# Linear attention's gate sums from edge rows by small DMAs, its steps reordered, and layer 0's denominators issued with the value matmuls

## The chip, the cores and the metric

The kernel runs on one core of a Trainium2 chip. The metric is device time in microseconds. The five engines each run their own instruction list in order: TensorE (PE, with its weight loads listed as PEld), VectorE (DVE), ScalarE (ACT), GpSimd (POOL) and SyncE (SP), which here issues most DMAs.

## The reference

A two-layer backbone over 2048 latent tokens and 256 context tokens of width 1024, all in float32. Layer 0 runs two groups of heads side by side: eight heads of softmax attention, and four heads of gated linear attention (GLA) in both directions. Layer 1 is a neighbourhood attention. The change lies in layer 0. GLA, for one direction, in chunks of tokens:

```python
def step(state, inp):
    qi, ki, vi, gi = inp                      # gi: log gates, one per key channel
    b = jnp.cumsum(gi, axis=-2)
    b_last = b[..., -1:, :]
    q_t, k_t = qi * jnp.exp(b), ki * jnp.exp(-b)
    att = jnp.where(mask, jnp.einsum('bhld,bhmd->bhlm', q_t, k_t), 0.0)
    o = jnp.einsum('bhld,bhde->bhle', q_t, state) + jnp.einsum('bhlm,bhme->bhle', att, vi)
    k_dec = ki * jnp.exp(b_last - b)
    state = state * jnp.exp(b_last)[..., 0, :, None] + jnp.einsum('bhld,bhle->bhde', k_dec, vi)
    return state, o
```

The softmax attention is the usual one: scores, exponential, sum over keys, value product, division by the sum (the denominator).

## The kernel before

All 2304 tokens stand as 18 tiles of 128, and GLA's chunk is one such tile. A tile framework traces the program and plans each engine's order from a modelled timeline: an instruction is placed when its inputs and a buffer are there in the model, those traced earlier first. `issue_after(x)` only keeps an instruction behind x on its engine. On the chip the lists are then fixed.

`even_mix` traces GLA's first pass and its scans (`gla`) and then softmax attention (`even_attention`), so the two are interleaved on all engines.

*Softmax attention.* Four pairs of heads `j`, each with a block of 256 context queries (2 key tiles) and four blocks of 512 queries (18 key tiles): 74 iterations for a pair, 296 in all. An iteration makes scores for two heads, three matmuls each (L1003 to L1005, tile `st`, three PSUM banks), two exponentials on ACT into `apt` (14 buffers), and two additions on DVE that sum the weights (L994, `acc`). Value matmuls (`tail`, L945, tile `av`, two banks) go out in groups: when six iterations are pending, four are issued (L1015). When a block's last value matmul has been issued, `late` receives the block with a countdown of iterations (L948); `step_late` counts down in every iteration (L1014), and at zero `finish` makes the denominators (L876, tile `den`, one bank), a logarithm and an exponential on ACT, three operations on DVE (L881 to L883, the last of which reads the `av` bank), and the gate on POOL (L885).

*GLA, first pass.* For a chunk, `front` loads its inputs `u`, makes three copies of the 32 low-rank gate inputs (POOL, L721), transposes them, makes gate logits and log gates `G` (one buffer). Then L739 makes cumulative sums `mid`, centred at the middle of the chunk, with the matrix `tri`. L743 makes the sums of each half of the chunk (four matmuls of two columns, weights `G`, moving `ind`), three activations take their exponentials into `fac`, and POOL multiplies them (L748). `qt` and `kt` (one buffer each) are the exponentials of `mid` and `-mid`, times q and k (L753). `back` transposes `qt` and `kt` (L766), makes scores (L776), masks them, makes the chunk's own output (L785), stored to DRAM, and the chunk's contribution to the state (L791), which DVE scales with `fac` into `D` (L792). All of it turns in two PSUM banks, tag `gl`. The three steps of `back` for a chunk alternate with the three of `front` for the next.

*GLA, scan and second pass.* `scan` runs over the 18 chunks, forward on POOL (half of the partitions) and backward on DVE (the other half), three operations a chunk (L814 to L816). The second pass multiplies the queries with each chunk's state (L835), normalises and gates. `hook` releases one step of it, and of the splitting of the next weights, in every fourth attention iteration from the 166th on.

SP issues all loads and stores of this stage in one list.

Of the kernel before, what the change touches and what calls it, by code (L numbers as in the profile page):

```python
# [10 lines left out]
F32 = mybir.dt.float32  # L11
# [77 lines left out]
class Kern:  # L89
# [596 lines left out]
    def gla(self, gp, gs, g1, gd, pp, tag):  # L686
# [5 lines left out]
        self.gO = self.scr("gO", (NT, P, 512), F32)  # L692
        raw = self.tl(gs, [P, 512], "ge")
# [7 lines left out]
        ind = self.tl(gp, [P, 2], "ind")  # L701
        nc.sync.dma_start(ind[:], self.i["halves"])
# [7 lines left out]
        fac = [self.tl(gp, [P, H, 3], f"fac{c}") for c in range(NT)]  # L710
# [3 lines left out]
        def front(c):  # L714

            u = self.tl(g1, [P, 1056], "gu")
            nc.sync.dma_start(u[:], self.Un[c, :, :1056])
            gq, gk, gv = u[:, :256], u[:, 256:512], u[:, 512:1024]
            ps = bank()
            u3 = self.tl(gs, [P, 3, 32], "gu3")  # L720
            g.tensor_copy(u3[:], u[:, 1024:1056].unsqueeze(1).to_broadcast([P, 3, 32]))  # L721
# [12 lines left out]
            nc.vector.scalar_tensor_tensor(out=G[:], in0=lg[:], scalar=0.0, in1=e[:], op0=ALU.min, op1=ALU.subtract)  # L734
            G4 = G[:].rearrange("p (h z d) -> p h z d", z=2, h=H)
            yield
            mid = bank()
            for z in range(2):
                nc.tensor.matmul(mid[:].rearrange("p (h z d) -> p h z d", z=2, h=H)[:, :, z, :], tri[:, z, :], G4[:, :, z, :], start=True, stop=True)  # L739
            hs = bank()  # L740
            hs4 = hs[:, : 2 * H].rearrange("p (h c) -> p h c", h=H)
            for h in range(H):
                nc.tensor.matmul(hs4[:, h, :], G[:, h * P : h * P + P], ind[:], start=True, stop=True)  # L743
            f = fac[c]
            self.act(f[:64, :, 0:2], hs4[:64], AF.Exp, scale=1 / 16)
            self.act(f[64:, :, 0], hs4[64:, :, 1], AF.Exp, scale=1 / 16)
            self.act(f[64:, :, 1], hs4[64:, :, 0], AF.Exp, scale=1 / 16)
            g.tensor_tensor(out=f[:, :, 2], in0=f[:, :, 0], in1=f[:, :, 1], op=ALU.mult)  # L748
            qt = self.tl(g1, [P, 512], "gqt", bufs=1)
            kt = self.tl(g1, [P, 512], "gkt", bufs=1)  # L750
            for dst, src, sc in ((qt, gq, 1 / 16), (kt, gk, -1 / 16)):
                self.act(dst[:], mid[:], AF.Exp, scale=sc)
                nc.vector.tensor_tensor(out=z4(dst[:]), in0=z4(dst[:]),  # L753
                                        in1=src.rearrange("p (h d) -> p h d", h=H).unsqueeze(2).to_broadcast([P, H, 2, 64]), op=ALU.mult)
            tiles[c] = gv, f, qt, kt
            yield

        def back(c):

            gv, f, qt, kt = tiles.pop(c)  # L760
# [7 lines left out]
            nc.sync.dma_start(self.gQ[c], qT[:].rearrange("p h t -> p (h t)"))  # L768
            yield
# [19 lines left out]
            ps = bank()  # L789
            for h in range(H):  # L790
                nc.tensor.matmul(ps[:, h * P : h * P + P], kt[:, h * P : h * P + P], gv[:, h * P : h * P + P], start=True, stop=True)  # L791
            nc.vector.tensor_tensor(out=Dl[c][:], in0=ps[:].rearrange("p (h t) -> p h t", h=H),  # L792
                                    in1=f[:, :, 1:2].to_broadcast([P, H, P]), op=ALU.mult)
            yield

        tiles = {}
        for _ in front(0):
            pass
        for c in range(NT):
            nxt = front(c + 1) if c + 1 < NT else iter(())  # L800
            for _ in back(c):
                next(nxt, None)

        def scan(order, sl, eng, name):
            S = None
            n = sl.stop - sl.start
            for c in order:
# [5 lines left out]
                else:  # L813
                    eng.tensor_tensor(out=N[sl], in0=S[sl], in1=f[sl, :, 2:3].to_broadcast([n, H, P]), op=ALU.mult)  # L814
                    eng.tensor_tensor(out=N[sl], in0=N[sl], in1=d[sl], op=ALU.add)  # L815
                    eng.tensor_tensor(out=d[sl], in0=S[sl], in1=f[sl, :, 0:1].to_broadcast([n, H, P]), op=ALU.mult)  # L816
# [72 lines left out]
    def even_attention(self, ap, pp, hook):  # L889
# [49 lines left out]
        def tail(j, nb, n, kt, pts):  # L939
# [7 lines left out]
            if n == len(kts) - 1:  # L947
                late.append([2 if nb else 5, j, nb])  # L948
# [15 lines left out]
        for j in range(4):  # L964
# [12 lines left out]
            for nb, (q0, w, kts) in enumerate(blocks):  # L977
# [18 lines left out]
                for n, kt in enumerate(kts):  # L996
# [823 lines left out]
```

## Time and profile before

| | us |
|---|---|
| median of 3 runs | 3648.87 (3647.48 to 3651.03) |
| profiled execution | 3651.72 |
| its span, first to last instruction | 3649.9 |
| mean granted TensorE clock | 0.985 |
| busy: PE / PEld / DVE / ACT / POOL | 3552.6 / 2750.0 / 2355.6 / 1433.1 / 1200.8 |

A row of the timeline gives start, duration, engine, line of the kernel, operation, tile written and tiles read, shapes, count, and in brackets how long the engine was idle before it and who released it. Matmuls overlap in their pipeline, so that the time from one start to the next says what one costs, not its duration. A float32 matmul shows as two records.

### The profile page before, as it was taken

Reading aid. Unit: us, or ns where it says so; the run is one execution under the profiler, and the core shown is the slowest. Engines: PE = TensorE matmul, PEld = TensorE weight load, DVE = VectorE, ACT = ScalarE, POOL = GpSimd, SP = SyncE. Lnnn points to the kernel's source line nnn. Section 1 sums busy time; section 2 is a strip of 40 time slices with the busy share of each in tenths; the row PEclk is TensorE's granted clock in tenths of the full one; section 3 lists DMA queues with packets and bytes.
Section 4 is the critical chain, followed back from the end, with each engine's and each line's share of the span. In section 5 each row is a group of like instructions: output and inputs, shape, how many; then the busy total and the mean of one; then the engine's idle time right before and its main releaser. Section 6 shows DMA issues by size and latency. Waiting matters only on the chain.

```text
span 3649.9 us, 51809 instructions
## 1 busy us (share of the span) xinstructions
PE 3552.6 (97%) x18404; PEld 2750.0 (75%) x18404; DVE 2355.6 (65%) x4860; ACT 1433.1 (39%) x2741; POOL 1200.8 (33%) x1336
## 2 busy tenths in 40 slices
PE   8999999999999999999999999999899999999899
PEld 6988998888886666665657878888688887555577
DVE  4677666888876666688664435545578784666721
ACT  5545551111115555555553224444422223555510
POOL 1433330101011222112311234333344434777743
PEclk9999999999999999999999999999999999999999
DMA  7455472222242232334533544445743437778554
GB/s 255 146 154 157 135 207 82 86 76 89 74 131 66 76 102 72 93 92 116 164 98 116 186 160 126 146 142 170 226 145 123 140 119 204 209 206 220 176 179 149
DMA packets 364372, 512.19 MB, mean 140 GB/s; under 512 B 25825, under 2 KB 243889, under 8 KB 358210
## 3 DMA queue, kind: packets, MB, share of 16 engines
q1 hardware_dynamic: 322642, 425.49, 39.5%
q0 software_dynamic: 19872, 55.92, 5.2%
q10 hardware_dynamic: 21600, 27.46, 2.1%
q8 instruction: 146, 2.39, 0.3%
q14 instruction: 112, 0.92, 0.1%
HBM read 329.38 MB, written 179.37 MB: 139 GB/s over the span
## 4 chain that ended last, share of the span: by engine, by line
PE 71%; issue 15%; DVE 5%; POOL 4%; DMA 4%; ACT 2%; POOLq 0%; SPq 0%; DVEq 0%; ACTq 0%
PE av L945 7%; PE gm L129 6%; PE gm L131 6%; PE gm L130 6%; PE st L1003 4%; PE st L1004 4%; PE st L1005 4%; PE o L1515 2%; PE st L129 2%; PE st L131 2%; PE st L130 2%; PE st L1482 2%; PE pj L129 2%; PE pj L131 2%; PE pj L130 2%
## 5 line engine op out<-in xcount | busy, mean ns | idle before, releaser
L994 DVE TENSOR_TENSOR acc<-acc,apt 128x512 f32<-128x512 f32 x512 | 368.7, 743 | 163.1 <-ACT apt L106 160.4
L106 ACT ACTIVATE apt<-st 128x512 f32<-128x512 f32 (+1 forms) x592 | 343.1, 593 | 290.8 <-PE st L1005 258.9
L662 DVE TENSOR_REDUCE mm<-mx 128x1 f32<-128x512 f32 (+1 forms) x656 | 393.0, 629 | 91.1 <-PE mx L661 82.8
L945 PE MATMUL av<-apt,av 128*64 128x512 f32 (+1 forms) x1184 | 279.1, 594 | 0.0
L1003 PE MATMUL st<-aq,akh 97*128 97x512 f32 x576 | 249.2, 433 | 4.2 <-ACT apt L106 4.2
L661 PE MATMUL mx<-mk,mq 96*128 96x512 f32 (+1 forms) x656 | 238.6, 372 | 0.0
L1004 PE MATMUL st<-aq,akh 96*128 96x512 f32 x576 | 230.0, 399 | 0.0
L1005 PE MATMUL st<-aq,akl 96*128 96x512 f32 x576 | 229.6, 399 | 0.0
L106 ACT ACTIVATE opt<-opt 128x930 f32<-128x930 f32 (+9 forms) x144 | 119.2, 830 | 247.9 <-POOL opt L1686 139.8
L1389 DVE CUSTOM_DVE_ANT_1 mx<-mx,mtab 128x217 f32<-128x217 f32 (+11 forms) x576 | 184.5, 338 | 49.5 <-PE mx L1383 37.0
L106 ACT ACTIVATE u<-gm 128x352 f32<-128x352 f32 (+1 forms) x144 | 70.3, 495 | 357.9 <-PE gm L131 208.2
L1646 DVE TENSOR_TENSOR opt<-st,tab 128x64 f32<-128x64 f32 (+10 forms) x576 | 142.8, 316 | 87.0 <-PE st L1483 60.7
L945 PEld LDWEIGHTS av<-apt,av 128*64 128x64 f32 x1184 | 80.4, 137 | 153.8 <-issue 152.2
L1521 POOL TENSOR_TENSOR oacc<-oacc,opt 128x682 f32<-128x682 f32 (+9 forms) x144 | 169.8, 1202 | 28.9 <-ACT opt L106 27.7
L1003 PEld LDWEIGHTS st<-aq,akh 97*128 97x128 f32 x576 | 109.3, 190 | 86.9 <-issue 45.0
L661 PEld LDWEIGHTS mx<-mk,mq 96*128 96x128 f32 x656 | 122.8, 188 | 11.7
L1005 PEld LDWEIGHTS st<-aq,akl 96*128 96x128 f32 x576 | 110.4, 192 | 25.4
L1004 PEld LDWEIGHTS st<-aq,akh 96*128 96x128 f32 x576 | 110.7, 192 | 17.5
L106 ACT ACTIVATE x<-px,modB,modA 128x128 f32<-128x128 f32 x272 | 99.1, 468 | 58.2 <-PE px L331 36.0
L1482 PE MATMUL st<-q,kt 128*128 128x480 f32 (+5 forms) x256 | 99.7, 391 | 22.5 <-DVE opt L1646 17.9
L815 POOL TENSOR_TENSOR gsf<-gsf,D 64x512 f32<-64x512 f32 x17 | 24.8, 1459 | 276.8 <-DVE D L792 276.8
L129 PE MATMUL gm<-w1h,hhi 128*128 128x512 f32 x288 | 115.1, 400 | 0.0
(576 smaller groups left out, 10020.6 us busy)
## 6 DMA issues: line engine op xcount, KB each, us to landing
q<-Q SPq DMA_DIRECT2D x48, 512.0 KB
H<-x ACTq DMA_DIRECT2D x36, 512.0 KB
adaw<-ada_w SPq DMA_DIRECT2D x64, 256.0 KB
x<-H SPq DMA_DIRECT2D x32, 512.0 KB
wraw<-w_od SPq DMA_DIRECT2D x64, 256.0 KB
K1t<-okt POOLq DMA_DIRECT2D x32, 512.0 KB, 7.7
kt<-K1t SPq DMA_DIRECT2D x32, 512.0 KB
mtab<-rpb_q SPq DMA_DIRECT2D x16, 899.0 KB
```

The lines of the kernel that those rows point to most:

```text
L106: return self.nc.scalar.activation(out, in_, func, **kw)
L129: self.nc.tensor.matmul(out, lh(k), rh(k), start=j == 0, stop=False)
L130: self.nc.tensor.matmul(out, lh(k), rl(k), start=False, stop=False)
L131: yield self.nc.tensor.matmul(out, ll(k), rh(k), start=False, stop=j == n - 1)
L661: mm = nc.tensor.matmul(ps[:, :w], q[:A_QK, (t % 6) * P : (t % 6) * P + P], k[:A_QK, k0 : k0 + w], start=True, stop=True)
L662: nc.vector.tensor_reduce(out=m[:, t, n : n + 1], in_=ps[:, :w], axis=AX.X, op=ALU.max)
L945: nc.tensor.matmul(O[j, nb][i * 64 : i * 64 + 64, :w], V[j, kt // TT][:, kt % TT, i * 64 : i * 64 + 64], pts[i][:, :w], start=n == 0, stop ...
L994: self.add = nc.vector.tensor_tensor(out=acc[i][:, :w], in0=a[:, :w], in1=pts[i][:, :w], op=ALU.add)
L1003: nc.tensor.matmul(ps[:, :w], kh[: A_QK + 1, i, kq], qh[: A_QK + 1, :w], start=True, stop=False)
L1004: nc.tensor.matmul(ps[:, :w], kh[:A_QK, i, kq], ql[:A_QK, :w], start=False, stop=False)
L1005: mm = nc.tensor.matmul(ps[:, :w], kl[:A_QK, i, kq], qh[:A_QK, :w], start=False, stop=True)
L1389: nc.vector.tensor_tensor_reduce(out=s, in0=s, in1=tb[:, ri : ri + rn, ci : ci + cn], scale=1.0, scalar=-3e38, op0=ALU.add, op1=ALU.max, a ...
```

## The change

The sums of the two halves of a chunk are already in the centred sums: the first and the last row of `exp(mid)` and `exp(-mid)` hold the exponentials of the halves' sums, up to the gate of the edge token itself. So the matmuls with `ind`, their bank and their activations go. Instead, two rows of `G`, one row each for two directions of `qt`, and two rows of `kt` are written to a small DRAM tensor `gE` before `qt` and `kt` are multiplied with q and k, and read back transposed into `fac`, one element per partition, head and kind. One exponential on ACT and two products on POOL finish the factors.

Around it the steps move. The multiplication with q and k goes from `front` to the start of `back`, and so does the load of `u`. The chunk's contribution to the state is made right after the transposes and copied by DVE; POOL multiplies it with its factor at the end of `back`. The three copies of the gate inputs come straight from a DMA. `front` runs up to two chunks ahead of `back`.

In softmax attention the countdown is 1 for every block, and `step_late` is called only when a value group goes out, ahead of it.

```diff
+        self.gE = self.scr("gE", (NT, 2, 3, 512), F32)
...
-        ind = self.tl(gp, [P, 2], "ind")
-        nc.sync.dma_start(ind[:], self.i["halves"])
...
-        fac = [self.tl(gp, [P, H, 3], f"fac{c}") for c in range(NT)]
+        fac = [self.tl(gp, [P, 4, H], f"fac{c}") for c in range(NT)]
...
         def front(c):
-            u = self.tl(g1, [P, 1056], "gu")
-            nc.sync.dma_start(u[:], self.Un[c, :, :1056])
-            gq, gk, gv = u[:, :256], u[:, 256:512], u[:, 512:1024]
             ps = bank()
             u3 = self.tl(gs, [P, 3, 32], "gu3")
-            g.tensor_copy(u3[:], u[:, 1024:1056].unsqueeze(1).to_broadcast([P, 3, 32]))
+            nc.sync.dma_start(u3[:], self.Un[c, :, 1024:1056].unsqueeze(1).to_broadcast([P, 3, 32]))
...
-            hs = bank()
-            hs4 = hs[:, : 2 * H].rearrange("p (h c) -> p h c", h=H)
-            for h in range(H):
-                nc.tensor.matmul(hs4[:, h, :], G[:, h * P : h * P + P], ind[:], start=True, stop=True)
-            f = fac[c]
-            self.act(f[:64, :, 0:2], hs4[:64], AF.Exp, scale=1 / 16)
-            self.act(f[64:, :, 0], hs4[64:, :, 1], AF.Exp, scale=1 / 16)
-            self.act(f[64:, :, 1], hs4[64:, :, 0], AF.Exp, scale=1 / 16)
-            g.tensor_tensor(out=f[:, :, 2], in0=f[:, :, 0], in1=f[:, :, 1], op=ALU.mult)
+            nc.sync.dma_start(self.gE[c, :, 2], G[0::127])
...
+            self.act(qt[:], mid[:], AF.Exp, scale=1 / 16)
+            for z, t in enumerate((127, 0)):
+                nc.sync.dma_start(self.gE[c, z : z + 1, 0], qt[t : t + 1])
+            self.act(kt[:], mid[:], AF.Exp, scale=-1 / 16)
+            nc.sync.dma_start(self.gE[c, :, 1], kt[0::127])
+            tiles[c] = qt, kt
+            yield
+
+        def back(c):
+            qt, kt = tiles.pop(c)
+            u = inputs.pop(c)
+            f = fac[c]
+            for z in range(2):
+                nc.sync.dma_start(f[z * 64 : z * 64 + 64, :3, :].rearrange("p n h -> p (n h)"),
+                                  self.gE[c, z].rearrange("n (h z d) -> z d (n h)", z=2, h=H)[z])
+            for dst, src in ((qt, gq), (kt, gk)):
                 nc.vector.tensor_tensor(out=z4(dst[:]), in0=z4(dst[:]), ...
...
             nc.sync.dma_start(self.gQ[c], qT[:].rearrange("p h t -> p (h t)"))
+            ps = bank()
+            for h in range(H):
+                nc.tensor.matmul(ps[:, h * P : h * P + P], kt[:, h * P : h * P + P], gv[:, h * P : h * P + P], start=True, stop=True)
+            nc.vector.tensor_copy(Dl[c][:].rearrange("p h t -> p (h t)"), ps[:])
             yield
...
             nc.sync.dma_start(self.gO[c], oi[:])
-            ps = bank()
-            for h in range(H):
-                nc.tensor.matmul(ps[:, h * P : h * P + P], kt[:, h * P : h * P + P], gv[:, h * P : h * P + P], start=True, stop=True)
-            nc.vector.tensor_tensor(out=Dl[c][:], in0=ps[:].rearrange("p (h t) -> p h t", h=H),
-                                    in1=f[:, :, 1:2].to_broadcast([P, H, P]), op=ALU.mult)
+            self.act(f[:, 2, :], f[:, 2, :], AF.Exp, scale=1 / 16)
+            g.tensor_tensor(out=f[:, 1, :], in0=f[:, 1, :], in1=f[:, 2, :], op=ALU.mult)
+            g.tensor_tensor(out=f[:, 3, :], in0=f[:, 0, :], in1=f[:, 1, :], op=ALU.mult)
+            g.tensor_tensor(out=Dl[c][:], in0=Dl[c][:], in1=f[:, 0, :].unsqueeze(2).to_broadcast([P, H, P]), op=ALU.mult)
             yield
...
-        for c in range(NT):
-            nxt = front(c + 1) if c + 1 < NT else iter(())
-            for _ in back(c):
-                next(nxt, None)
+        def fetch_u(c):
+            if c < NT:
+                inputs[c] = self.tl(g1, [P, 1056], "gu")
+                nc.sync.dma_start(inputs[c][:, :1024], self.Un[c, :, :1024])
+
+        tiles, inputs = {}, {}
+        fr = [front(c) for c in range(NT)] + [iter(())] * 2
+        fetch_u(0)
+        for c in (0, 0, 1, 0, 1):
+            next(fr[c])
+        for c in range(NT):
+            fetch_u(c + 1)
+            b = back(c)
+            for x in (b, fr[c + 2], fr[c + 1], b, fr[c + 2], b):
+                next(x, None)
...
             if n == len(kts) - 1:
-                late.append([2 if nb else 5, j, nb])
+                late.append([1, j, nb])
...
                     with self.tc.issue_after(mm.ins):
-                        step_late()
                         if len(pend) == 6:
+                            step_late()
                             for _ in range(4):
                                 tail(*pend.pop(0))
```

More of the change, by code (lines that the diff above doesn't have):

```diff
@@ L813, in scan @@
                 else:
-                    eng.tensor_tensor(out=N[sl], in0=S[sl], in1=f[sl, :, 2:3].to_broadcast([n, H, P]), op=ALU.mult)
+                    eng.tensor_tensor(out=N[sl], in0=S[sl], in1=f[sl, 3, :].unsqueeze(2).to_broadcast([n, H, P]), op=ALU.mult)
                     eng.tensor_tensor(out=N[sl], in0=N[sl], in1=d[sl], op=ALU.add)
-                    eng.tensor_tensor(out=d[sl], in0=S[sl], in1=f[sl, :, 0:1].to_broadcast([n, H, P]), op=ALU.mult)
+                    eng.tensor_tensor(out=d[sl], in0=S[sl], in1=f[sl, 1, :].unsqueeze(2).to_broadcast([n, H, P]), op=ALU.mult)
                 S = N
```

10 lines of the change are left out of this document (1 added, 9 removed).

## The prediction

> **What bounds it now.** I read the page first: the engines' shares, then the chain that ended last, then the DMA queues.
>
> ```profile
> PE 3552.6 (97%) x18404; PEld 2750.0 (75%) x18404; DVE 2355.6 (65%) x4860; ACT 1433.1 (39%) x2741; POOL 1200.8 (33%) x1336
> ...
> q1 hardware_dynamic: 322642, 425.49, 39.5%
> ...
> PE 71%; issue 15%; DVE 5%; POOL 4%; DMA 4%; ACT 2%; POOLq 0%; SPq 0%; DVEq 0%; ACTq 0%
> ```
>
> TensorE is busy for 97% of the span and holds most of the chain. The change touches layer 0's attention with the linear attention inside it, about 1084 to 1965 us, so I asked for busy time by stretches of 50 us there. Columns: stretch, its length, then PE, PEld, DVE, ACT and POOL busy, granted clock, DMA share, GB/s.
>
> ```profile
> 1300.00:1350.00 50.00, 50.00 (x262) 31.60 (x260) 32.33 (x48) 27.50 (x59) 11.52 (x12) 1.00 0.38 109
> ...
> 1650.00:1700.00 50.00, 45.83 (x202) 27.61 (x200) 45.94 (x69) 24.96 (x48) 9.47 (x9) 0.93 0.28 85
> ```
>
> At 1300 us PE has no gap, with DVE at 65% and ACT at 55%: here a microsecond of PE work removed is a microsecond off the end, and work moved to DVE, ACT, POOL or DMA is hidden while its queue isn't late. The second row is the exception: PE loses 4.2 us, the clock falls to 0.93, and DVE is at 92%.
>
> Next the instructions on the linear attention's PSUM banks, `gl` (duration min/median/max, then first and last start):
>
> ```profile
> L743 PE MATMUL gl<-ind,gG x144: 167/251/272, 1122.6 to 1583.4; 128*128 128x2 f32 x144
> L739 PE MATMUL gl<-gG,tri x72: 377/379/483, 1121.7 to 1579.6; 128*128 128x256 f32 x72
> ```
>
> The removed half-chunk sums are L743: 72 matmuls, two records each, four matmuls in each of 18 chunks. L739, which stays, gives the pace: (1579.6 - 1121.7) / 17 = 26.9 us a chunk.
>
> **1. The half-chunk matmuls go.** Their durations overlap, so the price is read from starts:
>
> ```profile
> 1312.14 0.40 PE L1005 MATMUL st<-aq,akl 96*128 96x512 f32 x1
> 1312.38 0.95 PE L743 MATMUL gl<-ind,gG 128*128 128x2 f32 x8
> 1313.19 0.48 PE L1003 MATMUL st<-aq,akh 97*128 97x512 f32 x1
> 1313.51 0.40 PE L1004 MATMUL st<-aq,akh 96*128 96x512 f32 x1
> ```
>
> From L1005 to the next L1004 it is 1.37 us; without the group two score matmuls in a row take 2 x 0.23 (rows below), so the group costs 0.90 with the dearer first matmul behind it, or 0.81 (1312.38 to 1313.19) where another group of this kind follows. I take 0.86: 18 x 0.86 = **-15.5 us** (14.6 to 16.2). Nothing covers it, since PE has no gap there.
>
> **2. Denominators join the value groups.**
>
> ```profile
> 1323.63 0.40 PE L1004 MATMUL st<-aq,akh 96*128 96x512 f32 x1
> 1323.86 0.40 PE L1005 MATMUL st<-aq,akl 96*128 96x512 f32 x1
> 1324.19 1.08 PE L876 MATMUL den<-acc,mtwos 128*64 128x512 f32 x4
> 1325.20 0.50 PE L1003 MATMUL st<-aq,akh 97*128 97x512 f32 x1
> 1325.54 0.40 PE L1004 MATMUL st<-aq,akh 96*128 96x512 f32 x1
> ...
> 1305.26 0.14 PEld L945 LDWEIGHTS av<-apt,av 128*64 128x64 f32 x2 [0.28 <-issue]
> 1305.69 0.14 PEld L945 LDWEIGHTS av<-apt,av 128*64 128x64 f32 x2 [0.28 <-issue]
> ```
>
> A denominator alone between scores costs 1325.54 - 1323.86 - 2 x 0.23 = 1.22 us. Inside a value group four such records (two heads, same 128x64 shape) take 2 x 0.43 = 0.86. The difference, 0.36, is the price of entering and leaving the 64-column shape. There are 20 blocks; the last keeps its place, and two may not find their group (step 4), so 17 x 0.36 = **-6.1 us** (3 to 6.8). If the planner puts other work between denominator and group, that one saves nothing.
>
> **3. The late scan.** The 4.2 us gap, from the timelines of DVE, ACT and PE:
>
> ```profile
> 1668.81 0.69 DVE L836 TENSOR_TENSOR goi<-gl,goi 128x512 f32<-128x512 f32 x1
> ...
> 1669.54 0.63 ACT L106 ACTIVATE ge<-goi 128x512 f32<-128x512 f32 x1 [5.48 <-DVE goi L836]
> ...
> 1665.45 1.08 PE L876 MATMUL den<-acc,mtwos 128*64 128x512 f32 x4
> 1670.71 0.79 PE L1003 MATMUL st<-aq,akh 97*128 97x512 f32 x1 [4.17 <-ACT apt L106]
> 1671.30 0.63 PE L1004 MATMUL st<-aq,akh 96*128 96x512 f32 x1
> ...
> 1676.12 4.26 PE L945 MATMUL av<-apt,av 128*64 128x512 f32 x16
> 1680.32 0.50 PE L1003 MATMUL st<-aq,akh 97*128 97x512 f32 x1
> ```
>
> DVE, still in the backward scan, reaches the second pass's first addition late; ACT stands 5.48 us on it in order, the exponentials behind it wait, and PE stops. Then score matmuls last 0.63 instead of 0.40 for some ten microseconds. From 1665.45 to 1680.32 it is 14.9 us; at full speed the same work is 1.0 (denominator) + 12 x 0.23 + 0.2 (shape changes) + 3.6 (value group) = 7.6. The loss is 7.3 us. Where the two meet, by tile:
>
> ```profile
> L835 PE MATMUL gl<-D,gqT x144: 275/275/377, 1661.6 to 1857.6; 128*128 128x128 f32 x144
> ...
> L816 DVE TENSOR_TENSOR D<-gsb,fac x17: 689/690/1420, 1179.3 to 1678.9; 64x512 f32<-64x512 f32 x17
> ```
>
> The second pass (L835) starts at a fixed attention iteration, and would come up by the 20 us saved ahead of it, to about 1641; the backward scan, now ending at 1679.6, starts when the last chunk is done. To be clear of each other the scan must end 39 us earlier: a chunk must take 2.2 us less than 26.9. The new order frees `gqt` and `gkt` (one buffer each) early, because the state matmul moves from the end of `back` to right behind the transposes; it works two chunks ahead, and one of ten bank uses a chunk goes. I take the whole **-7.3 us** (bounds -7.3 and 0). Finishing still earlier is worth nothing, because PE has attention to do all the while.
>
> **4. What the later denominators hold.** An output bank (`av`, two) is released by `finish`'s L883. In the normal case above, with the denominator at 1324.19:
>
> ```profile
> 1325.32 0.60 ACT L106 ACTIVATE rl<-den 128x512 f32<-128x512 f32 x1 [0.42 <-PE den L876]
> ...
> 1329.67 0.68 DVE L883 TENSOR_TENSOR rc<-av,rc 128x512 f32<-128x512 f32 x1
> ```
>
> Release comes at 1330.35, 6.2 us on. Groups go out at iterations 6, 10, 14, ...; the 74 iterations of a head pair put the pair's last large block and the next context block into one group (78), so both denominators now fall due at 82, right ahead of the value matmul that needs a third bank; before they were due at 80 and 83. Until release PE has the denominator (1.0) and, by three score banks and fourteen `apt` buffers, two and a half iterations of six matmuls (2.5 x 1.4 = 3.5): 1.7 us short, less what linear attention fills in. It happens at two of three pair changes (at 154 the two context value matmuls fill it): **+2 us**, between 0 and 2 x 8 (5.2 us of wait with nothing to fill it, and some 3 of slowed clock after, as in step 3). Rows show the slowed clock only behind 4.17 us of idle, so a stop of 1.7 might or might not bring it. The Trainium skill ("TensorE: Matmul & The Clock Gate", HAM oscillation) sets the limit at PE-idle gaps of about 3.4 us; by that rule short stops cost only themselves, and this step would end at 2 x 1.7 instead of 2 x 8.
>
> **5. Work moved off PE.**
>
> ```profile
> L792 DVE TENSOR_TENSOR D<-gl,fac 128x512 f32<-128x512 f32 x18 | 12.3, 685 | 7.1 <-PE gl L791 7.1
> L721 POOL COPY gu<-gu 128x96 f32<-128x96 f32 x18 | 10.0, 554 | 10.9 <-DMA gu<-Un 10.1 <-issue 0.8
> L848 POOL TENSOR_TENSOR goi<-goi,gsf 128x512 f32<-128x512 f32 x18 | 23.0, 1275 | 35.3 <-DVE goi L847 35.3
> ```
>
> DVE swaps a multiply for a copy of the same bank (0.69, the same). POOL loses 0.55 and gains one 128x512 multiply (1.3, the L848 row) and one tiny one per chunk. ACT loses two of its three tiny exponentials. Hidden: POOL is at 23% there. The cover's limit is that DVE lengthens while POOL runs:
>
> ```profile
> 1601.12 1.37 POOL L816 TENSOR_TENSOR D<-gsf,fac 64x512 f32<-64x512 f32 x1
> ...
> 1601.63 1.42 DVE L816 TENSOR_TENSOR D<-gsb,fac 64x512 f32<-64x512 f32 x1
> ```
>
> Against 0.69 otherwise: 18 x 0.7 = 13 us more DVE, spread over more than 300 us at 65%. Nothing.
>
> **6. The small DMAs**, per chunk on SP: `u3`, one for the rows of G, two for `qt`, one for `kt`, two for `f`. Seven, and 18 x 7 = 126 in all, against the one-off load of `ind` that goes.
>
> ```profile
> 1310.28 0.34 SPq L717 DMA_DIRECT2D gu<-Un  x1
> 1311.78 1.18 DVE L753 TENSOR_TENSOR gqt<-gqt,gu 128x512 f32<-128x512 f32 x1 [0.81 <-ACT gqt L106]
> 1318.40 0.27 POOL L721 COPY gu<-gu 128x96 f32<-128x96 f32 x1 [2.75 <-DMA gu<-Un]
> 1328.96 0.62 ACT L106 ACTIVATE goi<-gl 128x512 f32<-128x512 f32 x1
> ...
> M<-mr POOLq DMA_DIRECT2D x64, 2.0 KB, 2.4
> ```
>
> The multiplies L753 overwrite `qt` and `kt` in place, so on DVE they now wait until the edge rows have been read out. A 2 KB store takes 2.4 us; behind a burst of attention loads a load took 8.1 (1310.28 to 1318.40). Behind a waiting multiply on DVE stand the sums over `apt`; behind these, ACT's exponentials, then PE. The spare `apt` buffers and score banks cover about two iterations of 1.4 + 0.9 us. `f` is needed by ACT only behind `goi`, 17 us after the first multiply in this trace (1311.78 to 1328.96). `u3` reads only what layer 0 wrote long before. So most of it is hidden; I take +2.5 us, a third of step 3's loss once in the eighteen chunks; bounds 0 and the slower rivals below.
>
> **Sum.** -15.5 - 6.1 - 7.3 + 2 + 2.5 = -24.4 us. The profiled execution took 3651.72 (span 3649.9 and 1.8 around it), 0.08% above the median 3648.87 of three. 3651.72 - 24.4 = 3627.3; on the median's footing **3624.5**.
>
> **Rivals.**
> - *The scan still meets the second pass.* For: the planner works from modelled times, and with a bank ring of two the pace may stay near 26.9 us. Against: the single `gkt` is plainly held longest today. Step 3 then gives 0: 3648.9 - 17.1 = 3632.
> - *No difference.* New stops at pair changes (up to 16) or a few DVE holds eat the gain: 3642 to 3656, say 3648.
> - *Slower: DVE stands on edge rows behind a burst.* Place: the first multiply in `back`. SP's list is in one order; a row store planned behind attention loads lands up to 8 us late, and the sums wait. For: step 3 shows one late DVE costing 7.3 us with its slowed clock. Against: DMA share is only 0.38 there. From 24.4 / 7.3 = 3.3, so four held chunks of eighteen, the gain is gone. With six, 3624.5 + 6 x 7.3 = 3668.
> - *Slower: the `f` loads crowd the rings.* In `gE` the elements that one partition of `f` takes lie apart, so a load is 64 x 12 = 768 pieces. By the q1 row a piece takes at most 0.395 x 16 x 3650 / 322642 = 0.07 us on one engine: 3.4 us a load over 16 engines, 6.9 for two. The next chunk's edge rows queue behind them, so the hold grows from 2.4 to 9.3 us, 4.7 more than the two iterations of cover. In half the chunks: 3624.5 + 9 x 4.7 = 3667. Against: 0.07 is for pieces of 1.3 KB, and the two seldom follow at once. The Trainium skill ("DMA: Bandwidth & Descriptors", Rules for kernel authors) has the same mechanism: a non-contiguous last dimension becomes one descriptor per element. No row of this trace shows such a load.
>
> **How the numbers follow.** Forecast 0.50; scan still late 0.20; no difference 0.08; burst 0.13; crowded rings 0.09. A measurement of this kernel can tell 0.2%, 7.3 us, from no change: faster 0.70, same 0.08, slower 0.22. The forecast's own range is 3615 to 3634 (16.2 + 6.8 + 7.3 with no stops, plus a few us; or one more stop). To hold eight in ten, the range takes in the second and third case and the cheap end of the slower ones: 3612 to 3662.
>
> **What will show it.** L743's line is gone and the stretch stays at PE 50.00; denominators stand next to value groups; the last gate matmul comes well before 1580, no idle row of 4 us stands before a score matmul, and the clock stays 1.00 from 1650 to 1700. It is wrong if PE idle rows name ACT with DVE waiting on a DMA of `gE` before it, if matmuls of 0.63 turn up between 1120 and 1580, or if value groups wait on L883 for microseconds.

## The result, and the profile after

| | before | after |
|---|---|---|
| median us (range, runs) | 3649.95 (3647.48 to 3657.20, 4) | 3633.11 (3627.19 to 3635.74, 4) |
| profiled execution, span | 3651.72, 3649.9 | 3635.62, 3633.8 |

The change is faster by 16.8 us by the medians; the ratio is 0.9945, 95% interval 0.9932 to 0.9959. The forecast was 24.4 us. The page of the kernel after, its engines, the queue q1 and the chain:

```profile
PE 3525.9 (97%) x18260; PEld 2734.4 (75%) x18260; DVE 2355.6 (65%) x4860; ACT 1433.3 (39%) x2705; POOL 1221.2 (34%) x1354
...
q1 hardware_dynamic: 358138, 426.41, 40.6%
...
PE 68%; issue 15%; DVE 5%; DMA 5%; POOL 4%; ACT 3%; SPq 0%; POOLq 0%; DVEq 0%; ACTq 0%
```

TensorE still bounds it; DVE's total is the same to the tenth, and q1 has 35,496 packets more. To measure the stage that was changed I use two landmarks, the first context score matmul and the last denominator, in the instructions by tile (duration min/median/max, then first and last start). First the kernel before, then after:

```profile
L1003 PE MATMUL st<-aqc,akh x16: 281/322/471, 1084.5 to 1759.2; 97*128 97x256 f32 x16
L876 PE MATMUL den<-acc,mtwos x64: 592/593/644, 1143.2 to 1951.8; 128*64 128x512 f32 x64
```

```profile
L1012 PE MATMUL st<-aqc,akh x16: 281/287/388, 1089.8 to 1741.1; 97*128 97x256 f32 x16
L885 PE MATMUL den<-acc,mtwos x64: 592/592/643, 1150.4 to 1932.4; 128*64 128x512 f32 x64
```

The attention stage lasted 1951.8 - 1084.5 = 867.3 us and lasts 1932.4 - 1089.8 = 842.6: 24.7 us less. Not all of this is the change. The stage begins with a stop of 1.9 us, and behind it the clock is sometimes slowed. From PE's timeline of before, then of after:

```profile
1084.55 0.39 PE L1003 MATMUL st<-aqc,akh 97*128 97x256 f32 x1 [1.90 <-POOL akh L897]
...
1088.06 0.63 PE L1004 MATMUL st<-aq,akh 96*128 96x512 f32 x1
```

```profile
1089.77 0.39 PE L1012 MATMUL st<-aqc,akh 97*128 97x256 f32 x1 [1.90 <-POOL akh L906]
...
1093.22 0.40 PE L1012 MATMUL st<-aq,akh 97*128 97x512 f32 x1
```

The first 45 matmul records of the stage are the same work in the same order in all fourteen kernels of this document. From the first to the 46th they take 8.7 us in three of the profiles, 10.2 in five and 11.6 in six. I call this the start. Up to 2.9 us of a difference between two stages is the start and no effect of the kernel, so the table of the experiments lists it. Before has 10.2 and after 8.7; without the start the stage gained 23.2 us.

The rest of the span went from 2782.6 to 2791.2 us, though PE's order of work there is the same. In the profiled executions of the twelve experiments below, the rest lay between 2779.6 and 2786.1. So the two profiles differ by scatter outside the stage as well, and I use the stage, less its start where that differs, for what a part does, and the timed runs for what it is worth. The stage of after in stretches, columns as in the prediction:

```profile
1300.00:1350.00 50.00, 48.78 (x271) 31.07 (x268) 36.95 (x53) 27.51 (x55) 14.08 (x14) 1.00 0.47 111
1550.00:1600.00 50.00, 46.90 (x220) 29.47 (x219) 46.71 (x69) 23.04 (x41) 8.81 (x8) 0.93 0.25 71
...
1650.00:1700.00 50.00, 50.00 (x246) 31.75 (x241) 33.32 (x52) 28.93 (x61) 13.30 (x13) 1.00 0.43 117
```

The gap at 1650 us is gone. There is a new one of 3.1 us at 1550 with a clock of 0.93, and the ordinary stretch at 1300 is no longer without gaps. The new gap, from the timelines of DVE and PE:

```profile
1571.52 0.68 DVE L781 TENSOR_TENSOR ge<-gl,tri 128x512 f32<-128x512 f32 x1
1572.23 0.73 DVE L823 TENSOR_TENSOR gsb<-gsb,fac 64x512 f32<-64x512 f32 x1
1572.99 0.69 DVE L781 TENSOR_TENSOR gat<-gl,tri 128x512 f32<-128x512 f32 x1
1573.71 0.69 DVE L824 TENSOR_TENSOR gsb<-gsb,D 64x512 f32<-64x512 f32 x1
1574.43 0.69 DVE L783 TENSOR_TENSOR gat<-gat,ge 128x512 f32<-128x512 f32 x1
...
1571.77 0.40 PE L1014 MATMUL st<-aq,akl 96*128 96x512 f32 x1
1575.27 2.05 PE L787 MATMUL gl<-gu,gat 128*128 128x128 f32 x8 [3.10 <-DVE gat L783]
...
1577.54 0.63 PE L1013 MATMUL st<-aq,akh 96*128 96x512 f32 x1
...
1581.53 3.65 PE L954 MATMUL av<-apt,av 128*64 128x512 f32 x16
```

The backward scan (L823, L824) now starts before the last chunk is through, because the chunk's contribution to the state is made ahead of its scores; its steps stand in turn between that chunk's masks (L781, L783) on DVE, and the chunk's own output (L787) waits. From 1571.77 to 1581.53 are 9.76 us; the same work at full speed is an output group (0.81 to 0.9) and 13 score matmuls (13 x 0.23), 4 us: 5.7 lost. Next the pace, from the instructions by tile:

```profile
L735 PE MATMUL gl<-gG,tri x72: 377/378/483, 1123.7 to 1545.9; 128*128 128x256 f32 x72
```

A chunk takes (1545.9 - 1123.7) / 17 = 24.8 us instead of 26.9. And one group of the linear attention's scores (L778) in PE's timeline:

```profile
1295.91 1.03 PE L735 MATMUL gl<-gG,tri 128*128 128x256 f32 x4
1296.87 0.48 PE L778 MATMUL gl<-gqT,gkT 64*128 64x128 f32 x2
1297.28 0.50 PE L1012 MATMUL st<-aq,akh 97*128 97x512 f32 x1
...
1299.58 1.16 PE L778 MATMUL gl<-gqT,gkT 64*128 64x128 f32 x14
```

The 16 records are cut: one matmul (two records) goes out at once, the other seven 2.7 us later, after three heads' score matmuls. The group needs two banks; by the order of the bank uses the second one still holds the centred sums of L735, which ACT reads until 1298.06. Taken from start to start and added up over the stage, the groups that moved are (the last denominator up to the landmark):

| PE work in the stage | before us (groups) | after us (groups) |
|---|---|---|
| half-chunk sums | 15.4 (18) | 0 |
| scores of GLA | 21.7 (23) | 24.8 (30) |
| centred sums | 12.8 (18) | 15.1 (18) |
| gate logits | 4.4 (18) | 5.6 (18) |
| denominators | 22.1 (20) | 16.3 (20) |
| value groups | 273.0 (86) | 263.5 (80) |

Together they are 24.1 us less. The denominators before hold the 4.2 us stop. A joined one after reads (the view ends at 1389 us, inside the value group):

```profile
1387.46 1.08 PE L885 MATMUL den<-acc,mtwos 128*64 128x512 f32 x4
1388.37 1.03 PE L954 MATMUL av<-apt,av 128*64 128x512 f32 x4
```

0.91 from start to start, against 0.86 forecast, so that joining saves 0.31 of the 1.22 of a lone one, not 0.36. Sixteen of the twenty have a value matmul right behind them.

### The profile page after: what moved, and what is told of

The parts are those of the page before. It is cut to its first block, busy times and chain, and to the rows that moved or that the text cites. A ratio compares the mean times of both kernels' runs of the same rounds, so it can differ in the third digit from the quotient of the medians.

```text
span 3633.8 us, 51705 instructions
## 1 busy us (share of the span) xinstructions
PE 3525.9 (97%) x18260; PEld 2734.4 (75%) x18260; DVE 2355.6 (65%) x4860; ACT 1433.3 (39%) x2705; POOL 1221.2 (34%) x1354
## 4 chain that ended last, share of the span: by engine, by line
PE 68%; issue 15%; DVE 5%; DMA 5%; POOL 4%; ACT 3%; SPq 0%; POOLq 0%; DVEq 0%; ACTq 0%
PE av L954 7%; PE gm L129 6%; PE gm L130 6%; PE gm L131 6%; PE st L1012 4%; PE st L1013 4%; PE st L1014 4%; PE o L1524 2%; DMA wraw<-w_od 2%; PE st L129 2%; PE st L131 2%; PE st L130 2%; PE st L1491 1%; PE pj L131 1%; PE pj L129 1%
## 5 line engine op out<-in xcount | busy, mean ns | idle before, releaser
L1003 DVE TENSOR_TENSOR acc<-acc,apt 128x512 f32<-128x512 f32 x512 | 376.2, 764 | 151.6 <-ACT apt L106 147.9
L954 PE MATMUL av<-apt,av 128*64 128x512 f32 (+1 forms) x1184 | 269.2, 592 | 0.0
L1398 DVE CUSTOM_DVE_ANT_1 mx<-mx,mtab 128x225 f32<-128x225 f32 (+10 forms) x576 | 184.4, 338 | 45.1 <-PE mx L1392 36.4
L1530 POOL TENSOR_TENSOR oacc<-oacc,opt 128x682 f32<-128x682 f32 (+10 forms) x144 | 169.5, 1205 | 22.7 <-ACT opt L106 21.5
L1013 PEld LDWEIGHTS st<-aq,akh 96*128 96x128 f32 x576 | 110.3, 191 | 17.5
L129 PE MATMUL gm<-w0h,hhi 128*128 128x512 f32 x288 | 115.8, 402 | 0.0
```

Source lines behind the costliest of these rows:

```text
L129: self.nc.tensor.matmul(out, lh(k), rh(k), start=j == 0, stop=False)
L954: nc.tensor.matmul(O[j, nb][i * 64 : i * 64 + 64, :w], V[j, kt // TT][:, kt % TT, i * 64 : i * 64 + 64], pts[i][:, :w], start=n == 0, stop ...
L1003: self.add = nc.vector.tensor_tensor(out=acc[i][:, :w], in0=a[:, :w], in1=pts[i][:, :w], op=ALU.add)
L1013: nc.tensor.matmul(ps[:, :w], kh[:A_QK, i, kq], ql[:A_QK, :w], start=False, stop=False)
L1398: nc.vector.tensor_tensor_reduce(out=s, in0=s, in1=tb[:, ri : ri + rn, ci : ci + cn], scale=1.0, scalar=-3e38, op0=ALU.add, op1=ALU.max, a ...
```

## The experiments

"Stage" is the time between the two landmarks in the profiled execution; before has 867.3, after 842.6. "Start" is its first 45 matmul records; before has 10.2. Ratios are to the kernel before, timed on the same chip. Each edit makes the framework plan the order anew, so two kernels can differ in more places than the edit itself.

| kernel | median us | ratio, 95% interval | stage us | its start us |
|---|---|---|---|---|
| after | 3633.11 | 0.9945 (0.9932 to 0.9959) | 842.6 | 8.7 |
| half-chunk sums: out of the kernel before | 3646.24 | 0.9982 (0.9974 to 0.9991) | 863.9 | 11.6 |
| half-chunk sums: back in the new order | 3638.61 | 0.9971 (0.9961 to 0.9981) | 850.0 | 10.2 |
| edge DMAs out of after | 3631.62 | 0.9942 (0.9930 to 0.9954) | 846.6 | 11.6 |
| joined denominators alone | 3653.63 | 1.0013 (1.0004 to 1.0022) | 863.3 | 8.7 |
| all but the joined denominators | 3638.10 | 0.9965 (0.9952 to 0.9978) | 855.9 | 11.6 |
| before, second pass from 178 | 3643.57 | 0.9975 (0.9966 to 0.9985) | 861.2 | 11.6 |
| the same with joined denominators | 3643.07 | 0.9979 (0.9971 to 0.9988) | 855.0 | 8.7 |
| after, scan behind the mask | 3630.66 | 0.9949 (0.9937 to 0.9961) | 846.7 | 10.2 |
| and second pass from 170 | 3629.19 | 0.9939 (0.9927 to 0.9951) | 843.7 | 10.2 |
| and second pass from 174 | 3627.13 | 0.9936 (0.9922 to 0.9949) | 840.7 | 11.6 |
| that with the old denominators | 3640.99 | 0.9964 (0.9951 to 0.9978) | 855.4 | 10.2 |
| after, centred sums first | 3648.14 | 0.9993 (0.9985 to 1.0002) | 864.1 | 11.6 |

**The half-chunk sums, taken out of the kernel before.**

```diff
-            hs = bank()
-            hs4 = hs[:, : 2 * H].rearrange("p (h c) -> p h c", h=H)
-            for h in range(H):
-                nc.tensor.matmul(hs4[:, h, :], G[:, h * P : h * P + P], ind[:], start=True, stop=True)
...
-            self.act(f[:64, :, 0:2], hs4[:64], AF.Exp, scale=1 / 16)
```

> The kernel before without the 18 groups of half-chunk sums and their exponentials; the factors are constants of 1.0, so the gate factors are left out of the result, and nothing else. It prices step 1 in the old order. Theory as predicted: 18 groups of 0.86 us on a full TensorE come off whole, 15.5 us, so 3649.9 becomes about 3634. Rival: much of it is given back, as the kernel with the four half-sum matmuls put back into the new order was only 9.5 us slower than the changed kernel; then 3640 to 3644, with score groups of the linear attention cut in two more often than 23 groups for 18 chunks, because a group with three bank uses fewer between finds its second bank still held.

The ratio 0.9982 is 6.6 us of 3652, and the stage is 3.4 us shorter (4.8 without the start), though 15.4 us of PE work are gone. That is the rival, at the small end of its range. The score groups (L768 there) are cut 17 times in 18 (35 groups, 26.6 us from start to start, against 23 and 21.7), and PE waits more. Its waits in the stage (in total, times, longest), first of before, then of this kernel:

```profile
PE st L1003 <- ACT apt L106: 4.4, 2, 4.2
PE gl L766 <- DVE gqt L753: 0.2, 1, 0.2
```

```profile
PE st L995 <- ACT apt L106: 5.7, 3, 3.8
...
PE gl L758 <- DVE gkt L745: 1.5, 8, 0.2
PE gl L758 <- DVE gqt L745: 1.4, 3, 1.0
```

Without the stop at the first landmark, which both have, these are 8.6 us of waits against 4.6. The transposes (L758) reach DVE's gate multiplies too early once the half-chunk matmuls no longer stand between. Waits and cuts, 4.0 + 4.9, account for 8.9 of the 12.0 us by which the stage fell short, and the start for 1.4. That the missing group brought the waits and the cuts is read from these rows; no run takes away the held bank or the wait for DVE by itself.

**The half-chunk sums, put back into the new order** (and no edge rows):

```diff
-            nc.sync.dma_start(self.gE[c, :, 2], G[0::127])
+            hs = bank()
+            hs4 = hs[:, : 2 * H].rearrange("p (h c) -> p h c", h=H)
+            for h in range(H):
+                nc.tensor.matmul(hs4[:, h, :], G[:, h * P : h * P + P], ind[:], start=True, stop=True)
```

> The changed kernel with the half-chunk sums made by the four matmuls again (right behind the centred sums), and without the edge-row DMAs; order and denominators as changed. Theory, the removed matmuls carry the gain and the DMAs cost PE nothing: 15.5 us slower than the changed kernel, about 1 us faster than before. Rival, the reordering carries it: within 5 us of the changed kernel. Rival, the DMAs cost PE several us: 8 to 12 us slower than the changed kernel only.

It is 9.5 us slower than after (0.0026 of 3650), as the rival had it, though not for its reason, as the next kernel shows. The stage is 7.4 us longer (5.9 without the start), with 15.1 us in the group. The score groups are whole again (23, 21.7 us) and the longest stop is 2.6 us instead of 3.1. So in either order the eighteen groups cost PE 15 us and are worth 6 to 10 by time. I read this as the use of the bank and of the microsecond that they put between the centred sums and the scores; no run separates the two. Against the kernel with joined denominators alone, which differs from this one by the order of GLA's steps and what moved with it (the scaling of `D` to POOL, the copies of the gate inputs to a DMA), it has 850.0 to 863.3 in the stage, and 0.9971 to 1.0013 by time: the order with these is worth 13 to 15 us.

**The edge DMAs, taken out of after.**

```diff
-            nc.sync.dma_start(self.gE[c, :, 2], G[0::127])
...
-            for z in range(2):
-                nc.sync.dma_start(f[z * 64 : z * 64 + 64, :3, :].rearrange("p n h -> p (n h)"),
-                                  self.gE[c, z].rearrange("n (h z d) -> z d (n h)", z=2, h=H)[z])
```

> The changed kernel without the stores of edge rows, the loads of the factors and the products made of them; the factors are constants of 1.0, so the gate factors are left out of the result. Theory (step 6, the small DMAs and their holds cost 2.5 us): 3630.6 against 3633.1, and the same 20-odd idle microseconds that ACT spends on the factors' loads gone without PE noticing. Rival: the DMAs and the waits on them eat the missing half of step 1, so this kernel is 6 to 10 us faster than the changed one, 3623 to 3627.

1.5 us faster by the medians, 0.9942 to 0.9945, and a stage 4.0 us longer, of which the start is 2.9: no difference that could be told. What they cost in after shows on ACT and DVE, not on PE (waits from 1085 to 1650 us, of ACT and of DVE):

```profile
ACT fac L106 <- DMA fac<-gE: 24.1, 18, 3.7
```

```profile
DVE gqt L757 <- DMA gE<-gqt: 5.0, 3, 2.0
```

ACT stands 24.1 us on the factors over the eighteen chunks, and without that the time is the same.

**The denominators.** Alone on the kernel before:

```diff
-                late.append([2 if nb else 5, j, nb])
+                late.append([1, j, nb])
...
-                        step_late()
                         if len(pend) == 6:
+                            step_late()
```

> The kernel before with the denominators' change alone (countdown 1, step_late only with a value group). Theory: an own entry into the 64-column shape costs 0.36 us, 17 of them go, and the 4.2 us stop in the scan stays: 6 us faster than before, about 0.17%. Rival, that the join is worth more because value groups are also interrupted less often: 10 us or more faster. Rival, that the output banks held longer give it back: 0 to 2 us.

The theory fell in the timed runs: 1.0013, 4.7 us slower, where the stage of the profile is 4.0 us shorter (2.5 without the start). The stop of the late scan is 5.3 us there instead of 4.2, and the stretch from 1650 us has less PE time and a lower clock than in before:

```profile
1650.00:1700.00 50.00, 44.71 (x198) 27.36 (x196) 40.90 (x64) 24.45 (x48) 9.21 (x9) 0.90 0.33 90
```

So I took the late scan away first. The kernel before, with the second pass later:

```diff
-                    if count[0] >= 166 and count[0] % 4 == 2:
+                    if count[0] >= 178 and count[0] % 4 == 2:
```

> The kernel before, with the second pass (and the preparation of weights that shares its steps) begun at the 178th attention iteration instead of the 166th, some 30 us later: it then starts behind the end of the backward scan. It prices step 3 by itself. Theory: the stop of 4.17 us and the slowed clock behind it are gone, 7.3 us in all, so about 3643 against 3650. Rival: DVE is as full as before and another wait takes the stop's place, as in the two kernels that moved the scan of the changed kernel; then 3647 to 3651.

0.9975, 9.1 us, with the stage 6.1 us shorter (7.5 without the start); 7.3 were forecast for the stop and what follows it. The stretch is full:

```profile
1650.00:1700.00 50.00, 50.00 (x220) 29.06 (x218) 45.75 (x71) 28.50 (x49) 3.58 (x3) 1.00 0.27 72
```

DVE is as busy (45.75 against 45.94), and no other wait took the stop's place. Then the joined denominators on top of it:

> The same later second pass together with the changed placing of the denominators alone. It prices step 2 where the late scan is out of the way. Theory (step 2, 6.1 us less a stop or two at pair changes): 4 to 6 us faster than the later second pass alone, 3637 to 3639. Rival: the joined denominators are worth nothing or less by themselves, as the kernel with them alone was 0.13% slower than before; then 3643 to 3648.

The stage goes from 861.2 to 855.0, 6.2 us, which looks like step 2, but 2.9 of these are the start: 3.3 are left. From start to start, score matmuls and denominators do lose 6.2 us beside the start, and other groups (value groups 1.2 us, transposes of gate inputs 1.5) take nearly half of it back. The times are the same, as the rival had it: 3643.57 and 3643.07, with ratios 0.9975 and 0.9979. On top of the new order, from 0.9965 without to 0.9945 with them, it is 7.3 us, though these two intervals overlap:

> The changed kernel with the denominators put back as they were (countdown 2 or 5, step_late in every iteration). Theory: the linear attention part alone is worth what is left of the 16.8 us measured, about 11 us faster than before (0.3%). Rival, that the denominators carry most of it: 5 us or less.

And with the scan out of the way in the new order:

> The kernel with the scan behind the mask and the second pass at the 174th iteration, with the denominators placed as before. It prices step 2 a third time, in the order of work without a late scan. Theory (step 2): 6 us and more slower than with the joined denominators, so 3633 to 3637 against 3627.1, with the attention stage longer by the same. Rival: the stage is longer by 6 us or more, and the times agree within 3 us all the same, as they did in the old order; then the gain of step 2 in the stage is lost elsewhere, and the landmarks ahead of and behind the attention should show about 2781 us here against 2785.

0.9964 against 0.9936, 10.2 us, and 14.7 in the stage (16.1 without the start). Here the old place costs more than the shape changes. The waits of its scores and outputs, then those of the scores with the joined ones:

```profile
PE st L1013 <- ACT apt L106: 4.3, 4, 1.7
...
PE gl L787 <- DVE gat L783: 1.6, 4, 0.8
```

```profile
PE st L1013 <- ACT apt L106: 0.5, 2, 0.3
```

All waits inside the stage are 6.4 us here and 4.2 with the joined ones, so waits are a small part. The larger one is that other work breaks up the score matmuls: they stand in 242 runs here and in 192 with the joined ones, and take 455.0 against 443.4 us from start to start. In the old order it is 224 against 196 runs. Why the planned order breaks them up so much more here is not shown.

Why the joined denominators show in the time in the new order and not at all in the old is open. The rest of the span does not settle it: outside the stage the pair in the new order has 2783.4 and 2784.6 us (old place, joined), the pair in the old order 2780.6 and 2785.6, all within the scatter above. Over the fourteen profiles, those with joined denominators have 2785.0 us there on average and those with the old place 2781.4, so a part may be lost there; single profiles don't show it.

**The scan in the kernel after.** First held behind the last chunk's mask:

```diff
-            nc.vector.tensor_tensor(out=at[:], in0=at[:], in1=t2[:], op=ALU.add)
+            self.masked = nc.vector.tensor_tensor(out=at[:], in0=at[:], in1=t2[:], op=ALU.add)
...
-        scan(self.back_order(), slice(64, 128), nc.vector, "gsb")
+        with self.tc.issue_after(self.masked.ins):
+            scan(self.back_order(), slice(64, 128), nc.vector, "gsb")
```

> The changed kernel with the backward scan on DVE kept behind the last chunk's mask addition. In the changed kernel DVE makes scan steps ahead of that mask, PE stands 3.1 us on it and then runs at a slower clock, 5.7 us in all. Theory: the stop goes, 5 to 6 us faster than the changed kernel, 22 us faster than before. Rival, DVE is simply too full while the scan runs, and another wait takes its place: within 2 us of the changed kernel.

The rival held, 0.9949 against 0.9945 for after. The stop at the mask is gone, and the old one is back some 75 us later. From PE's and ACT's timelines:

```profile
1651.45 0.79 PE L1013 MATMUL st<-aq,akh 97*128 97x512 f32 x1 [4.43 <-ACT apt L106]
```

```profile
1650.28 0.63 ACT L106 ACTIVATE ge<-goi 128x512 f32<-128x512 f32 x1 [4.73 <-DVE goi L846]
```

It is the row of the prediction's step 3, `ge<-goi` behind DVE's addition. With the second pass later as well, from the 170th and the 174th iteration (the edit of one number shown above):

> The changed kernel with the backward scan kept behind the last chunk's mask, and the second pass begun four attention iterations later (from the 170th instead of the 166th). Theory (step 3, a late scan costs 5 to 7 us through DVE, ACT and PE in turn): neither meeting is left, no idle row of 3 us or more stands before a matmul between 1550 and 1700 us, the clock stays 1.00 there, and it is 5 to 7 us faster than the changed kernel, 3626 to 3628. Rival: DVE is full from 1560 to 1650 whatever comes first, another engine's turn behind it is late instead, and the time stays at 3630 to 3633 as when the scan alone was held.

> The changed kernel with the backward scan behind the last chunk's mask and the second pass begun at the 174th iteration. Theory: begun at the 170th it still left one stop of 2.0 us before a score matmul and a granted clock of 0.97 in 1650 to 1700 us; eight iterations later nothing is left of either, and it is 6 to 8 us faster than the changed kernel, 3625 to 3627. Rival: the later second pass costs at its own end what it saves at its start, and the time stays at 3629 to 3633.

From 170 a stop of 2.0 us is left (its row is in the last section), and the time lies between the theory and the rival; from 174 no stop over 0.8 is left behind the first microseconds of the stage. The stretches from 174:

```profile
1550.00:1600.00 50.00, 50.00 (x242) 30.55 (x238) 46.97 (x69) 24.94 (x45) 7.80 (x8) 1.00 0.32 90
1600.00:1650.00 50.00, 50.00 (x215) 29.75 (x214) 48.36 (x73) 29.53 (x50) 1.67 (x1) 1.00 0.16 43
1650.00:1700.00 50.00, 50.00 (x237) 30.01 (x236) 38.86 (x60) 29.01 (x57) 11.74 (x11) 1.00 0.46 124
```

3627.13 is the lowest median of all; it beats the kernel before by 0.64%. Against after (0.9936 to 0.9945) it is 3.3 us where 6 to 8 were forecast, and the intervals overlap; the stage is 1.9 us shorter (4.8 without the start). The waits were two places of one conflict: DVE is full from about 1560 to 1650, and what PE needs of it there is late.

**The cut scores.** A chunk's centred sums ahead of the next transpose:

```diff
-            for x in (b, fr[c + 2], fr[c + 1], b, fr[c + 2], b):
+            for x in (b, fr[c + 1], fr[c + 2], b, fr[c + 2], b):
```

> The changed kernel with one thing moved: a chunk's centred sums come ahead of the next chunk's transpose, instead of behind it, so that the score pair which follows takes the bank of the sums first released. In the changed kernel 12 of the 18 score groups are cut into one matmul and seven; a cut costs about 0.44 us (24.8 against 21.7 us over 30 and 23 groups). Theory: the cuts are gone or nearly, and 3 to 5 us with them, 3628 to 3630. Rival: the second bank is then held by the next chunk's transpose, the cuts stay, and the time stays within 3 us of 3633.

Both were wrong: by the medians it is 15 us slower than after, by the ratios 17.5. The groups are cut 17 times (35), and the stage is 21.5 us longer (18.6 without the start), with waits all over it:

```profile
PE st L1012 <- ACT apt L106: 5.7, 4, 3.6
PE gl L787 <- DVE gat L783: 4.6, 9, 2.9
```

Swapping two neighbours in the order of steps costs nearly the whole gain of the change. What a cut costs by itself was not measured; an order of steps that keeps the groups whole without the half-chunk matmuls was not found.

## Why the prediction was right, and where not

The direction and the range held, and the stage gained 24.7 us against 24.4 in the sum. That agreement is luck: 1.5 us of it are the start, and the terms miss both ways and cancel. A path from before to after in three kernels, by stage and by time, against the terms:

| step | stage us | without the start | time us (ratio x 3650) | forecast |
|---|---|---|---|---|
| denominators (before to joined alone) | -4.0 | -2.5 | +4.7 | -6.1 and +2 |
| order of GLA's steps, and what moved with it | -13.3 | -14.8 | -15.3 | -7.3 |
| edge rows for half-chunk matmuls | -7.4 | -5.9 | -9.5 | -15.5 and +2.5 |

**Step 1, the matmuls: mis-sized.** The price of a group was right (15.4 measured, 15.5 forecast); the sentence that failed is "Nothing covers it, since PE has no gap there". A full PE shows that the group takes time, not that what follows is ready earlier. By the rows above, without it the scores meet a bank still held and the transposes meet DVE: 6.6 us came off in the old order, 9.5 in the new. The prediction counted the bank use that goes as a help for the pace; the pace without the group in the old order is (1579.5 - 1123.1) / 17 = 26.8 us, unchanged, read from this row of that kernel:

```profile
L739 PE MATMUL gl<-gG,tri x72: 377/379/483, 1123.1 to 1579.5; 128*128 128x256 f32 x72
```

**Step 2, the denominators: about half in the stage of the old order, open in the time.** 3.3 us there of 6.1 forecast, with 16 joined of 17 forecast. The price was near (0.31 for each that is joined, against 0.36), but other groups took part of it back, and the sum had no term for that. Two stand alone between scores, in after at changes of head pairs (1323 and 1754 us), as step 4 had it. In time 0 or a loss in the old order, 7 to 10 us in the new.

**Step 3, the late scan: price and mechanism right, gain not had.** 9.1 us by time and 7.5 in the stage without the start when only that is removed, 7.3 forecast. The pace came out as needed, and the scan ended (1644) before the second pass began (1651.7). What failed is "Finishing still earlier is worth nothing": the earlier scan met the last chunk's masks on DVE, 5.7 us lost. One of the prediction's signs of being wrong came with it, matmuls of 0.63 between 1120 and 1580 (from 1577.54). Whether the stop would return in another place was asked only for the second pass. The order's larger gain, 13 to 15 us, was not in the sum at all: the prediction gave the order no effect but this one. Value groups are broken up less often (88 in the kernel with joined denominators alone, 77 with the new order, 273.6 to 263.0 us).

**Step 4, the output bank: smaller than taken.** In after no value group waits for an output bank; 2 us were taken, and up to 16 feared. The 0.7 us below is for the denominators' own bank, which L891 reads. PE's waits in the stage of after, then the one wait of a value group, in the kernel without the edge DMAs at the second change of head pairs (1564 us):

```profile
PE gl L787 <- DVE gat L783: 3.1, 1, 3.1
PE gl L778 <- DVE rT L721: 2.2, 3, 0.7
...
PE gl L764 <- DVE gG L730: 0.8, 1, 0.8
...
PE den L885 <- DVE rc L891: 0.7, 1, 0.7
```

```profile
PE av L946 <- DVE rc L884: 2.0, 1, 2.0
```

There the mechanism shows, near the 1.7 us of the step.

**Step 5: nearly right.** DVE's total is unchanged, POOL's 20 us higher. On PE 3.0 us of short waits behind DVE (for `rT` and `gG`, rows above) are new in the stage, where nothing was forecast.

**Step 6, the DMAs: right.** Forecast 2.5, measured 1.5, which the intervals do not tell from nothing. The rival of crowded rings falls: q1's share rose by 1.1 points for 11% more packets, and SP issues a factor load of 768 pieces in 0.63 us at the median (row by tile):

```profile
L754 SPq DMA_DIRECT2D fac<-gE x36: 607/630/1526, 1127.8 to 1550.6; - x36
```

The rival of the burst falls too: DVE waited 3 times of 18, at most 2.0 us. The cover that step 6 saw on ACT was not there: with 17 us counted on, ACT waited for the factors in all eighteen chunks, 24.1 us in sum, and PE did not notice.

**Why the runs show 17 to 20 and the stage 25.** Of the 24.7, 1.5 are the start. And the profile of after has 8.6 us more outside the stage than that of before, ahead of it 5.3 (first landmark 1089.8 against 1084.5). Kernels with the same work ahead have their first landmark between 1083.2 and 1087.7, so after's profile is the late one of them; no cause for it is shown.

## What to carry to other kernels

A group of matmuls on a full engine is worth its start-to-start time only if what stands behind it is ready that much earlier; look for the bank and the other engine that the next group needs before taking the whole price. When a wait sits in a stretch where a second engine is full (here DVE, 46 to 49 of 50 us), speeding up what leads to it moves the wait to the next thing that needs that engine; start the consumer later instead. When steps on a planned timeline are reordered, price the whole order by an experiment, since a swap of two neighbours moved the time by 15 to 18 us. Before a difference of a few microseconds between two profiles is put down to a change, compare a stretch that is the same in both: here such a stretch differed by up to 2.9 us.

## What the runs showed of the hardware

The slowed clock comes behind shorter stops than the 4.17 us that the prediction named. The trace of the kernel before already had it behind 1.90 us (rows in the section on the result). In the kernel with the second pass from 170, PE's timeline:

```profile
1657.77 0.50 PE L1013 MATMUL st<-aq,akh 97*128 97x512 f32 x1 [1.98 <-ACT apt L106]
...
1658.61 0.63 PE L1013 MATMUL st<-aq,akh 97*128 97x512 f32 x1
...
1661.99 0.40 PE L1015 MATMUL st<-aq,akl 96*128 96x512 f32 x1
```

1.98 us of idle, and 0.8 us later some 3.4 us of matmuls at 0.63 instead of 0.40, which costs 1.5 us more. The same idle time does not always do it. The stop of 1.9 us at the start of the stage is in all fourteen profiles, with the same release (POOL) and the same 45 records behind it: these ran at full speed in three, lost 1.5 us in five and 2.9 in six. By the rule of the Trainium skill that step 4 weighed ("TensorE: Matmul & The Clock Gate", HAM oscillation), only gaps above about 3.4 us matter; these rows do not agree, and the measurement decides.
